# Where a two-layer mixer block computes its modulation vectors: from VectorE alone to TensorE in layer 0

## The chip, the core and the metric

One core of one Trainium2 chip runs the whole program as one launch. The metric is the device time of one execution in microseconds. Five engines work beside each other: TensorE (PE in the profile, with its weight loads as PEld), VectorE (DVE), ScalarE (ACT), GpSimd (POOL) and SyncE (SP), which here only issues transfers.

## The reference, cut to what matters

Two layers work on 256 context rows and 256 latent rows of width 1024. Each layer first turns two conditioning vectors (`c` and `c_ctx`, one row each) into six modulation vectors of 1024 (shift, scale and gate for the mixer, then for the feed-forward part):

```
sc_, scc = silu(c), silu(c_ctx)
mx_ = sc_ @ w_ada[l] + b_ada[l]          # 1024 x 6144 weights, 24 MB a layer
mc_ = scc @ w_ada[l] + b_ada[l]
sx1, ax1, gx1, sx2, ax2, gx2 = split(mx_, 6)
hx = rmsnorm(x, g_pre_mix[l]) * (1 + ax1) + sx1
yc, yx = token_mixer(hc, hx, ...)        # mLSTM, HGRN2 and differential attention on projections h @ w_in
x = x + gx1 * rmsnorm(yx, g_post_mix[l])
hx = rmsnorm(x, g_pre_ffn[l]) * (1 + ax2) + sx2
x = x + gx2 * rmsnorm(swiglu(hx, ...), g_post_ffn[l])
```

The context rows go the same way in layer 0 and are only read in layer 1, so layer 1 needs both vectors for its first two parts and only the latent one for the rest.

## The kernel before, in words

Rows sit 128 to a tile (four tiles: context 0 and 1, latent 2 and 3). All large products run on TensorE in three passes: weights are split into a rounded part and a rest (`whi`, line 295 on ScalarE; `wlo`, line 296 on VectorE), the activations `hT` likewise, and line 300 issues hi·hi, lo·hi and hi·lo. Weights come in blocks of 512 KB or less through a ring of three raw buffers (`wload`, loads issued by SP at line 292) into two split buffers each.

The stages of a layer, in the order of the program: a first projection; HGRN2 (`hg_proj`, `hg_mix`, heads in pairs, lines 735 to 866), whose mixing is a chain of small matmuls, copies on ScalarE and products on VectorE; the attention's projections (evacuated at line 904 with a bias row that SP loads at line 621); the attention itself (`da_tile`, lines 958 to 995), run in lockstep with mLSTM's decay factors (`ml_W`); mLSTM's projections; mLSTM (`ml_half`); the output projection; the feed-forward part.

The program is not executed in that order on each engine. The framework plans the engines' instruction streams ahead: at each point of its plan an engine takes the instruction that stands earliest in the program among those it deems ready, so later projections (line 300) fill the holes of the mixers. On the chip every engine, and SP's queue, then runs its own stream strictly in that order and waits where an operand is late.

**Modulation before.** The columns of layer 0's first two vectors are computed by TensorE in the opening stage (`first_mod`, line 489), as each `lhsT` is the 32-column block of `csil` that holds the two conditioning vectors. All others come from `ada_group` (line 195), a generator that is advanced by `ada_step` once for each weight block of a projection. A step loads 128 rows by 1024 columns of `w_ada` (512 KB, line 210, ring `araw` of two) and adds it, times one scalar for each partition, onto an accumulator of 128 x 1024 for each of the one or two vectors (`kinds`): line 224 for the first, line 226 for the others, on VectorE. After eight steps a gather on TensorE (line 231) sums the accumulator over partitions by multiplying with a 0/1 selector of 32 columns, into 32-partition strips of a PSUM bank of its own (`psa`), and VectorE adds the bias (line 233). Gate vectors are multiplied by their norm gain on GpSimd and put in DRAM; the others are transposed (line 247).

Layer 0's groups 1 (mixer gate) and 2 (feed-forward shift and scale) run during layer 0's mixers; their accumulators take the place of the residual rows `R`, which are loaded a second time afterwards (`load_rows`, line 1179). Group 3 (feed-forward gate) and layer 1's groups 0 to 3 are appended at line 1211, and their steps belong to the feed-forward part, though the plan starts the first of them earlier.

The eight PSUM banks are four for projections (`mm`), three for mixers (`mx`) and one for the modulation. The profile writes one float32 matmul as two instructions, so the counts of lines 231 and 489 are twice the program's.

Of the kernel before, what the change touches and what calls it, by code (L numbers as in the profile page):

```python
# [10 lines left out]
F32 = mybir.dt.float32  # L11
# [4 lines left out]
ALU = mybir.AluOpType  # L16
AX = mybir.AxisListType

P = 128
D = 1024  # L20
# [55 lines left out]

NPT = 2

NMM = 4

HP1, AHEAD = 20, 2000
# [18 lines left out]
def dit_block(ctx: ExitStack, tc: tile.TileContext, x, c, ctx_in, c_ctx, w_ada, b_ada, g_pre_mix,  # L100
# [12 lines left out]
    sm = pool("sm", 2)  # L113
    stg = pool("stg")
    psm = pool("psm", NMM, space=bass.MemoryType.PSUM)
    psx = pool("psx", 7 - NMM, space=bass.MemoryType.PSUM)
    psa = pool("psa", 1, space=bass.MemoryType.PSUM)
    drp = pool("drp", 1, space=bass.MemoryType.DRAM)

    uid = [0]  # L120
# [74 lines left out]
    def ada_group(l, g, place):  # L195


        c01 = ADA_COLS[g]
        kinds = (0, 1) if l < DEPTH - 1 or g == 0 else (0,)
        ns = 2 * len(c01)  # L200
        ba = par.tile([P, 512], F32, tag="ba", name=nm("ba"))
        G.memset(ba, 0.0)
        for r in range(2):
            for i, c0 in enumerate(c01):
                SY.dma_start(out=ba[64 * i + r:64 * i + r + 33:32, :], in_=b_ada[l, c0:c0 + D].rearrange("(j n) -> j n", j=2))
        todo = [(i, k) for i in range(len(c01)) for k in range(KD)]

        def load(i, k):
            raw = wp.tile([P, D], F32, tag="araw", name=nm("araw"), bufs=2)
            SY.dma_start(out=raw, in_=w_ada[l, k * P:(k + 1) * P, c01[i]:c01[i] + D])  # L210
            return raw

        raws = [load(*todo[0])]
        accs = {}
        for n_, (i, k) in enumerate(todo):
            if n_ + 1 < len(todo):
                raws.append(load(*todo[n_ + 1]))
            raw = raws.pop(0)
            if k == 0:
                accs[i] = place(kinds)  # L220
            for r in kinds:
                a = accs[i][r]
                if k == 0:
                    V.tensor_scalar_mul(a, raw, csil[:, k, r:r + 1])
                else:
                    V.scalar_tensor_tensor(out=a, in0=raw, scalar=csil[:, k, r:r + 1], in1=a, op0=ALU.mult, op1=ALU.add)  # L226
            yield
        ps = psa.tile([P, 512], F32, tag="ada", name=nm("ada"))
        for r in kinds:
            for j in range(ns):  # L230
                PE.matmul(ps[32 * j:32 * j + 32, :], lhsT=esel[:, r, :], rhs=accs[j // 2][r][:, (j % 2) * 512:(j % 2 + 1) * 512],
                          start=r == 0, stop=r == kinds[-1], skip_group_check=True)
        V.tensor_add(ba[:32 * ns], ps[:32 * ns], ba[:32 * ns])
        if g % 2:
            gp = par.tile([64, 512], F32, tag="gp", name=nm("gp"))
            G.memset(gp, 0.0)
            for r in range(2):
                SY.dma_start(out=gp[r:r + 33:32, :], in_=(g_post_mix, g_post_ffn)[g // 2][l].rearrange("(j n) -> j n", j=2))
            G.tensor_tensor(gp, gp, ba[:64], op=ALU.mult)
            gd = drp.tile([2, D], F32, tag=f"gd{l}{g}", name=nm("gd"))  # L240
            for j in range(2):
                G.dma_start(out=gd[:, j * 512:(j + 1) * 512], in_=gp[32 * j:32 * j + 2, :])
            ggd[l, g // 2] = gd
        else:
            pt = pst([P, 4, P])
            for c_ in range(4):
                PE.transpose(pt[:, c_, :], ba[:, c_ * P:(c_ + 1) * P], ident)
            cm = par.tile([P, 4, 4, 2], F32, tag=f"adaC{g}", name=nm("adaC"))
            V.tensor_copy(cm, vap(pt, 0, [[P, 4], [32, 4], [1, 2]]))
            adaC[l, g] = cm  # L250
        yield


# [20 lines left out]
    def ada_flush():  # L274
        while pending:
            ada_step_now()
# [201 lines left out]
    def first_mod(k):  # L478
        aw = aw0
        if k > 0:  # L480
            aw = ep.tile([P, KD, 2, P], F32, tag="aw", name=nm("aw"), bufs=4)
            for i in range(2):
                load_aw(aw, k, i)
        if k % 2 == 0:
            w0s[k // 2] = wload(first_src(0)[k // 2], eng=G)
        ps = psa.tile([P, 256], F32, tag="ada", name=nm("ada"))
# [106 lines left out]
    for l in range(DEPTH):  # L593
# [3 lines left out]
        q0 = qt[0] * P  # L597
        halves = (1, 0) if full else (1,)
        if full:

            turn = [0]

            def place0(kinds):
                turn[0] ^= 2
                return {r: res.tile([P, D], F32, tag=f"R{turn[0] + r}", name=nm("acc")) for r in kinds}
            pending += [ada_group(0, g, place0) for g in (1, 2)]
        mst = ExitStack()
        Y = {t: yp.tile([P, D], F32, tag=f"Y{t}", name=nm("Y")) for t in qt}
        mix = mst.enter_context(tc.tile_pool(name=f"mix{l}", bufs=1, reuse_waits="tile"))

        class Bias:

            def __init__(self, parts, p_, bufs=1):
                self.parts, self.row, self.pool, self.bufs = parts, None, p_, bufs

            def load(self):
                if self.row is None:
                    self.row = self.pool.tile([P, 512], F32, tag="brow", name=nm("brow"), bufs=self.bufs)
                    o = 0
                    for p in self.parts:  # L620
                        SY.dma_start(out=self.row[:, o:o + p.shape[-1]], in_=p.partition_broadcast(P))
                        o += p.shape[-1]

            def __getitem__(self, sl):
                return self.row[sl]
# [28 lines left out]
        hst = ExitStack()  # L654
        hg = hst.enter_context(tc.tile_pool(name=f"hg{l}", bufs=1, reuse_waits="tile"))
        Vhg = hg.tile([P, 4, 256], F32, tag="Vhg", name=nm("Vhg"))
        b0 = Bias([b_in[l, c0:c0 + n] for c0, n in first_cols] + [ml_f_bias[l]], hg)
        if l == 0:
            b0.row = b0_first

        def b0_load():
            if l > 0:
# [205 lines left out]
        ml_gates()  # L868
        lockstep(hg_mix(0), hg_mix(1))
        hg_out(0)  # L870
        bg = Bias([b_in[l, O_HGV + 256:O_HGV + 512]], hg)

        def ev_g(tt, ps):

# [153 lines left out]
        def chain(*gens):  # L1028
            for g in gens:
                yield from g  # L1030

        def spaced(gen, n):

            for _ in gen:
                for _ in range(n):
                    yield

        w_all = spaced(chain(*[ml_W(h, 1) for h in range(ML_H)]), WSP)
        if full:
            lockstep(chain(da_tile(2), da_tile(0)), chain(da_tile(3), da_tile(1)), w_all)  # L1040
        else:
            lockstep(da_tile(2), da_tile(3), w_all)
        def ev_v(t, ps, bb):
            V.tensor_tensor(Vml[:, t, :, :ML_D], ps.rearrange("p (h d) -> p h d", h=ML_H), bb.rearrange("p (h d) -> p h d", h=ML_H),
                            op=ALU.add)
# [156 lines left out]
        if l + 1 < DEPTH:  # L1202
            accq = stg.tile([P, 4, 768], F32, tag="qk", name=nm("accq"))
            turn1 = [0]

            def place1(kinds):
                turn1[0] ^= 1
                if turn1[0]:
                    return {r: vap(accq, D * r, [[1, D]]) for r in kinds}
                return {r: ff.tile([P, D], F32, tag="acc", name=nm("acc")) if r else vap(accq, 2 * D, [[1, D]]) for r in kinds}  # L1210
            pending += [ada_group(l, 3, place1)] + [ada_group(l + 1, g, place1) for g in range(4)]
        with tc.tile_pool(name=f"ff{l}", bufs=1, reuse_waits="tile") as ff:
            y_T(halves[-1], (0, 1))
            out_rest(halves[-1])
# [102 lines left out]
```

## Time and profile before

| | us |
|---|---|
| median of three runs | 1362.05 |
| lowest and highest of them | 1360.01, 1362.66 |
| the profiled execution, its own time | 1362.45 |
| its span in the trace | 1360.7 |
| TensorE busy | 1273.4 |
| VectorE busy | 895.8 |
| ScalarE busy | 609.0 |
| GpSimd busy | 197.7 |

The span is the stretch from the first to the last recorded instruction; the profiled execution's own time is 1.75 us longer than that. The mean granted TensorE clock is 0.975 of full speed.

How to read it: a busy time is the union of an engine's instructions, and a matmul counts until its result is out, so back-to-back matmuls overlap. Waits are put down to what came last by the trace.

### The profile page before, as it was taken

The numbers are of one execution on the slowest core, as the hardware profiler recorded it, in microseconds if no ns is written. First come the engines' busy times: TensorE is split into PE (matmuls) and PEld (weight loads), VectorE is DVE, ScalarE is ACT, GpSimd is POOL, SyncE is SP. The second block draws the span as 40 slices with busy tenths as digits, with TensorE's granted clock in tenths as the row PEclk, the third lists the DMA queues.
The fourth block names the chain that finished last, engine by engine and source line by source line (L and its number), as shares of the span: only waits on it lengthen the run. The fifth ranks groups of instructions, "written<-read, shape, count | busy, mean of one in ns | idle before, by whom it ended". The sixth has DMA issues, their size and how long they took to land. (4 is left out here: it accounts for less than half of the span.)

```text
span 1360.7 us, 21798 instructions
## 1 busy us (share of the span) xinstructions
PE 1273.4 (94%) x8414; PEld 1071.2 (79%) x8414; DVE 895.8 (66%) x1552; ACT 609.0 (45%) x1147; POOL 197.7 (15%) x304
## 2 busy tenths in 40 slices
PE   7998995999999899999999999899889998999997
PEld 5776874778878698788887887777787796899996
DVE  4899996665688898576436347667837666555555
ACT  3436451458544563222221236546425745544443
POOL 3123202111242300001000003132111111000001
PEclk9999997999999899999999999899889999899999
DMA  9872525222334577587425334531332424466563
GB/s 279 247 210 64 171 76 160 64 73 75 125 101 139 180 225 253 159 260 242 132 93 181 99 109 146 137 103 45 83 94 61 119 78 130 118 185 186 186 187 123
DMA packets 144309, 193.96 MB, mean 143 GB/s; under 512 B 10604, under 2 KB 110230, under 8 KB 144206
## 3 DMA queue, kind: packets, MB, share of 16 engines
q1 hardware_dynamic: 142782, 188.89, 46.0%
q0 software_dynamic: 1424, 3.68, 0.8%
q8 instruction: 66, 1.08, 0.3%
q14 instruction: 37, 0.30, 0.1%
HBM read 191.47 MB, written 1.08 MB: 142 GB/s over the span
## 5 line engine op out<-in xcount | busy, mean ns | idle before, releaser
L295 ACT CAST whi<-wraw 128x1024 fp32r<-128x1024 f32 (+3 forms) x259 | 259.2, 1001 | 456.4 <-PE mm L300 432.5
L296 DVE TENSOR_TENSOR wlo<-wraw,whi 128x1024 fp32r<-128x1024 f32 (+3 forms) x255 | 298.4, 1172 | 212.9 <-PE mm L300 115.6
L300 PE MATMUL mm<-hT,whi 128*128 128x256 f32 (+1 forms) x1920 | 357.1, 337 | 1.7 <-ACT whi L295 0.6
L300 PEld LDWEIGHTS mm<-hT,whi 128*128 128x128 f32 x1920 | 296.9, 192 | 41.7 <-issue 4.0
L300 PE MATMUL mm<-whi,hT 128*128 128x384 f32 (+4 forms) x1152 | 262.9, 358 | 10.3 <-DVE qk L904 5.0
L300 PEld LDWEIGHTS mm<-whi,hT 128*128 128x128 f32 x1152 | 198.8, 192 | 43.2 <-issue 12.1
L300 PE MATMUL mm<-hT,wlo 128*128 128x256 f32 (+1 forms) x960 | 185.5, 335 | 0.0
L300 PEld LDWEIGHTS mm<-hT,wlo 128*128 128x128 f32 x960 | 150.4, 191 | 17.6 <-issue 0.4
L300 PE MATMUL mm<-wlo,hT 128*128 128x384 f32 (+4 forms) x576 | 140.3, 353 | 0.0
L300 PE MATMUL mm<-whi,GT 128*128 128x512 f32 x504 | 127.4, 392 | 0.5 <-ACT whi L295 0.5
L300 PEld LDWEIGHTS mm<-whi,GT 128*128 128x128 f32 x504 | 93.6, 188 | 22.4 <-ACT whi L295 2.2
L300 PEld LDWEIGHTS mm<-wlo,hT 128*128 128x128 f32 x576 | 100.7, 191 | 12.0 <-issue 5.7
L226 DVE SCALAR_TENSOR_TENSOR accq<-araw,csil,accq 128x1024 f32<-128x1024 f32 x63 | 80.9, 1294 | 27.7 <-DMA araw<-in_w_ada_dram 27.4
L300 PE MATMUL mm<-wlo,GT 128*128 128x512 f32 x252 | 67.9, 389 | 0.0
L226 DVE SCALAR_TENSOR_TENSOR acc<-araw,csil,acc 128x1024 f32<-128x1024 f32 x49 | 62.9, 1307 | 4.1 <-DMA araw<-in_w_ada_dram 4.0
L300 PEld LDWEIGHTS mm<-wlo,GT 128*128 128x128 f32 x252 | 47.3, 188 | 9.9
L410 POOL TENSOR_SCALAR rstd<-hss 128x1 f32<-128x1 f32 (+2 forms) x44 | 19.6, 444 | 221.1 <-ACT hsq L634 139.1
L1249 DVE TENSOR_TENSOR sg<-sg,mm 128x256 f32<-128x256 f32 (+1 forms) x48 | 24.8, 519 | 34.6 <-PE mm L300 33.9
L411 POOL TENSOR_TENSOR rstd<-rstd,mhalf 128x1 f32<-128x1 f32 (+2 forms) x58 | 46.2, 797 | 4.7
L1273 POOL TENSOR_TENSOR Z<-Z,gg 128x512 f32<-128x512 f32 x6 | 8.9, 1491 | 234.2 <-ACT sqz L1272 234.2
L973 ACT ACTIVATE e<-mx,damx 128x512 f32<-128x512 f32 (+1 forms) x48 | 29.3, 616 | 26.0 <-DVE damx L970 25.9
L968 DVE TENSOR_REDUCE damx<-mx 128x1 f32<-128x512 f32 (+1 forms) x48 | 28.1, 597 | 18.8 <-PE mx L966 18.2
(275 smaller groups left out, 1466.3 us busy)
## 6 DMA issues: line engine op xcount, KB each, us to landing
araw<-in_w_ada_dram SPq DMA_DIRECT2D x80, 512.0 KB
wraw<-in_w_ffn_down_dram SPq DMA_DIRECT2D x50, 512.0 KB
wraw<-in_w_ffn_gate_dram SPq DMA_DIRECT2D x48, 512.0 KB
wraw<-in_w_ffn_up_dram SPq DMA_DIRECT2D x48, 512.0 KB
wraw<-in_w_in_dram SPq DMA_DIRECT2D x36, 512.0 KB
wraw<-in_w_in_dram SPq DMA_DIRECT2D x36, 384.0 KB
wraw<-in_w_out_dram SPq DMA_DIRECT2D x24, 512.0 KB
aw<-in_w_ada_dram SPq DMA_DIRECT2D x16, 512.0 KB
```

The costliest lines, as they stand in the source:

```text
L226: V.scalar_tensor_tensor(out=a, in0=raw, scalar=csil[:, k, r:r + 1], in1=a, op0=ALU.mult, op1=ALU.add)
L295: S.copy(hi[:, :nk, :n], raw[:, :nk, :n])
L296: (eng or V).tensor_tensor(lo[:, :nk, :n], raw[:, :nk, :n], hi[:, :nk, :n], op=ALU.subtract)
L300: PE.matmul(ps, lhsT=lhs, rhs=rhs, start=first, stop=last, skip_group_check=True)
L410: G.tensor_scalar(o[:, :width], ss, 1.0 / n, EPS, ALU.mult, ALU.add)
L411: G.tensor_tensor(o[:, :width], o[:, :width], mhalf[:, :width], op=ALU.pow)
L968: V.reduce_max(mx[:, j:j + 1], ps[:, :nk], axis=AX.X)
L973: S.activation(e[:, j, :nk], pp[j][:, :nk], AF.Exp, bias=mx[:, 2 + j:3 + j], scale=sc, accum_out=mx[:, 4 + j:5 + j])
L1249: V.tensor_mul(sg[:, :n], sg[:, :n], ps)
L1273: (V if cb else G).tensor_tensor(zs, zs, gg[1 if t < 2 else 0][:, cs_], op=ALU.mult)
```

## The change

Layer 0's four modulation vectors that are not computed in the opening stage go back to TensorE, in a new generator `ada_group0`: it takes two column blocks at once, loads 128 x 512 pieces (256 KB, ring of four) and issues for each a float32 matmul with `csil[:, k, :]` (32 columns) as `lhsT`, four pieces into the four 32-partition strips of one `mx` bank, accumulated over the eight steps k. Both gates (group 0) are stepped from the projections, one step for every second weight block (`pace[1] = 2`); shift and scale of the feed-forward part (group 1) are stepped from the attention's lockstep, one step for each three rounds. There is no accumulator in SBUF, so `R` stays and the second `load_rows` goes.

Layer 1's groups stay on VectorE, with loads and products cut into halves of 512 columns (ring of four) and two further steps (`LAG`) between the last product and the gather. They now come first in the feed-forward part, as layer 0's group 3 is gone from there.

The modulation's own PSUM bank becomes a fourth `mx` bank, which opening stage, gathers and `ada_group0` share with the mixers. Two bias rows move: layer 1's first one to `yp`'s tile `Y0`, HGRN2's gate bias to the staging tile `qk`.

```diff
-    psx = pool("psx", 7 - NMM, space=bass.MemoryType.PSUM)
-    psa = pool("psa", 1, space=bass.MemoryType.PSUM)
+    psx = pool("psx", 8 - NMM, space=bass.MemoryType.PSUM)
...
-        todo = [(i, k) for i in range(len(c01)) for k in range(KD)]
+        todo = [(i, k, h) for i in range(len(c01)) for k in range(KD) for h in range(2)]
...
-            raw = wp.tile([P, D], F32, tag="araw", name=nm("araw"), bufs=2)
+            raw = wp.tile([P, 512], F32, tag="araw", name=nm("araw"), bufs=4)
...
+            if h:
+                yield
+        for _ in range(LAG):
             yield
-        ps = psa.tile([P, 512], F32, tag="ada", name=nm("ada"))
+        ps = pst([P, 512])
...
+    def ada_group0(g):
+
+        c01 = ((2 * D, 5 * D), (3 * D, 4 * D))[g]
...
+        ps = pst([P, 512])
+        for k in range(KD):
+            for j in range(4):
+                raw = wp.tile([P, 512], F32, tag="araw", name=nm("araw"), bufs=4)
+                SY.dma_start(out=raw, in_=w_ada[0, k * P:(k + 1) * P, c01[j // 2] + (j % 2) * 512:c01[j // 2] + (j % 2) * 512 + 512])
+                PE.matmul(ps[32 * j:32 * j + 32, :], lhsT=csil[:, k, :], rhs=raw, start=k == 0, stop=k == KD - 1, skip_group_check=True)
+            if k < KD - 1:
+                yield
+        V.tensor_add(ba, ps, ba)
+        if g == 0:
+            for i in range(2):
+                gate_store(0, i, ba, i)
+        else:
+            norm_cols(0, 2, ba)
+        yield
...
-            pending += [ada_group(0, g, place0) for g in (1, 2)]
+            pending.append(ada_group0(0))
+            pace[1] = 2
...
-        b0 = Bias([b_in[l, c0:c0 + n] for c0, n in first_cols] + [ml_f_bias[l]], hg)
-        if l == 0:
-            b0.row = b0_first
+        b0 = Bias([b_in[l, c0:c0 + n] for c0, n in first_cols] + [ml_f_bias[l]],
+                  row=b0_first if full else yp.tile([P, D], F32, tag="Y0", name=nm("b0")))
...
-        bg = Bias([b_in[l, O_HGV + 256:O_HGV + 512]], hg)
+        bg = Bias([b_in[l, O_HGV + 256:O_HGV + 512]], row=vap(stg.tile([P, 4, 768], F32, tag="qk", name=nm("bg")), 0, [[1, 256]]))
...
+        ada_flush()
+        ada_rest = spaced(ada_group0(1), 2) if full else iter(())
...
-            lockstep(chain(da_tile(2), da_tile(0)), chain(da_tile(3), da_tile(1)), w_all)
+            lockstep(chain(da_tile(2), da_tile(0)), chain(da_tile(3), da_tile(1)), ada_rest, w_all)
...
+        for _ in ada_rest:
+            pass
...
-        if full:
-            load_rows()
...
-            pending += [ada_group(l, 3, place1)] + [ada_group(l + 1, g, place1) for g in range(4)]
+            pending += [ada_group(l + 1, g, place1) for g in range(4)]
+            pace[1] = 1
```

## Rows read from the trace of the kernel before

**Rows 1.** Page of the profile, part 1: engines over the whole span
```profile
PE 1273.4 (94%) x8414; PEld 1071.2 (79%) x8414; DVE 895.8 (66%) x1552; ACT 609.0 (45%) x1147; POOL 197.7 (15%) x304
```

**Rows 2.** Windows: stretch, length, PE PEld DVE ACT POOL busy (instructions), PEclk, DMA, GB/s
```profile
55.00:205.00 150.00, 141.34 (x1618) 111.69 (x1619) 142.01 (x239) 74.49 (x135) 31.68 (x27) 0.99 0.45 137
205.00:225.00 20.00, 5.82 (x21) 2.49 (x21) 16.18 (x28) 2.53 (x3) 7.44 (x9) 0.70 0.61 186
225.00:365.00 140.00, 136.69 (x738) 112.38 (x737) 78.17 (x189) 78.65 (x200) 23.04 (x55) 0.99 0.26 77
365.00:480.00 115.00, 106.55 (x589) 87.76 (x588) 94.70 (x193) 60.74 (x143) 38.50 (x54) 0.94 0.47 150
480.00:845.00 365.00, 362.18 (x1755) 299.81 (x1755) 220.19 (x243) 117.52 (x157) 18.24 (x20) 1.00 0.55 174
845.00:1160.00 315.00, 285.36 (x2030) 243.54 (x2028) 202.86 (x444) 164.73 (x356) 57.44 (x101) 0.95 0.34 95
```

**Rows 3.** Who waited for whom, TensorE, 55 to 370 us: total, times, longest
```profile
PE ada L231 <- DVE acc L226: 14.2, 1, 14.2
...
PE mx L798 <- ACT Ck L789: 3.7, 3, 2.4
```

**Rows 4.** Timeline around 210 us, all engines: start, length, engine, line, operation
```profile
198.91 10.04 SPq L210 DMA_DIRECT2D araw<-in_w_ada_dram  x4
...
215.24 0.90 SPq L621 DMA_DIRECT2D brow<-in_b_in_dram  x2
...
219.30 0.33 SPq L210 DMA_DIRECT2D araw<-in_w_ada_dram  x1
...
222.05 2.48 DVE L904 TENSOR_TENSOR qk<-mm,brow 128x512 f32<-128x512 f32 x4
...
222.18 1.93 PE L231 MATMUL ada<-acc,esel 128*32 128x512 f32 x6 [14.19 <-DVE acc L226]
...
224.04 5.11 PE L300 MATMUL mm<-whi,hT 128*128 128x512 f32 x16
...
230.80 3.79 PE L300 MATMUL mm<-whi,hT 128*128 128x512 f32 x16
```

**Rows 5.** Timeline, the same place in layer 1
```profile
994.58 2.50 PE L300 MATMUL mm<-whi,hT 128*128 128x320 f32 x8 [5.01 <-DVE qk L904]
```

**Rows 6.** Busy time by stretch of line 226 alone
```profile
55.00:250.00 195.00, 53.97 (x42) 0.96 0.45 137
250.00:480.00 230.00, 20.26 (x16) 0.97 0.36 111
```

**Rows 7.** Busy time of line 231 alone, all of layer 0's groups
```profile
100.00:460.00 360.00, 10.11 (x32) 1.46 (x32) 0.97 0.35 107
```

**Rows 8.** Timeline at 572 us, a gather of eight matmuls in one run
```profile
571.86 1.06 PE L231 MATMUL ada<-accq,esel 128*32 128x512 f32 x8
...
573.71 1.21 PE L300 MATMUL mm<-whi,GT 128*128 128x512 f32 x4
```

**Rows 9.** Timeline of TensorE, gathers among softmax rounds (280 us) and alone (444 us)
```profile
279.96 1.06 PE L231 MATMUL ada<-acc,esel 128*32 128x512 f32 x6
...
280.94 0.80 PE L300 MATMUL mm<-whi,hT 128*128 128x384 f32 x3
...
444.44 1.04 PE L231 MATMUL ada<-accq,esel 128*32 128x512 f32 x2
...
445.42 0.73 PE L300 MATMUL mm<-whi,hT 128*128 128x512 f32 x2
```

**Rows 10.** Who waited for whom, VectorE, 55 to 250 us
```profile
DVE acc L226 <- DMA araw<-in_w_ada_dram: 4.0, 4, 1.6
DVE acc L224 <- DMA araw<-in_w_ada_dram: 0.6, 1, 0.6
```

**Rows 11.** Who waited for whom, TensorE, 370 to 850 us
```profile
PE mx L439 <- DVE nsc L447: 2.1, 1, 2.1
...
PE mm L300 <- DVE hT L1133: 1.4, 1, 1.4
```

More of the change, by code (lines that the diff above doesn't have):

```diff
@@ L77 @@
 NPT = 2
+LAG = 2
 NMM = 4
@@ L205, in ada_group, with load @@
                 SY.dma_start(out=ba[64 * i + r:64 * i + r + 33:32, :], in_=b_ada[l, c0:c0 + D].rearrange("(j n) -> j n", j=2))
-        todo = [(i, k) for i in range(len(c01)) for k in range(KD)]
-        def load(i, k):
-            raw = wp.tile([P, D], F32, tag="araw", name=nm("araw"), bufs=2)
-            SY.dma_start(out=raw, in_=w_ada[l, k * P:(k + 1) * P, c01[i]:c01[i] + D])
+        todo = [(i, k, h) for i in range(len(c01)) for k in range(KD) for h in range(2)]
+        def load(i, k, h):
+            raw = wp.tile([P, 512], F32, tag="araw", name=nm("araw"), bufs=4)
+            SY.dma_start(out=raw, in_=w_ada[l, k * P:(k + 1) * P, c01[i] + 512 * h:c01[i] + 512 * h + 512])
             return raw
-        raws = [load(*todo[0])]
+        raws = [load(*x_) for x_ in todo[:3]]
         accs = {}
-        for n_, (i, k) in enumerate(todo):
-            if n_ + 1 < len(todo):
-                raws.append(load(*todo[n_ + 1]))
+        for n_, (i, k, h) in enumerate(todo):
+            if n_ + 3 < len(todo):
+                raws.append(load(*todo[n_ + 3]))
             raw = raws.pop(0)
-            if k == 0:
+            if k == h == 0:
                 accs[i] = place(kinds)
             for r in kinds:
-                a = accs[i][r]
+                a = accs[i][r][:, 512 * h:512 * h + 512]
                 if k == 0:
@@ L234, in ada_group @@
         if g % 2:
[L235 to L242, printed above, removed]
@@ L243, in ada_group, with gate_store @@
-            ggd[l, g // 2] = gd
-        else:
[L245 to L250, printed above, removed]
+            gate_store(l, g // 2, ba, 0)
+        else:
+            norm_cols(l, g, ba)
+        yield
+    def gate_store(l, which, ba, i):
+        o = 64 * i
+        gp = par.tile([P, 512], F32, tag="gp", name=nm("gp"))
+        G.memset(gp, 0.0)
+        for r in range(2):
+            SY.dma_start(out=gp[o + r:o + r + 33:32, :], in_=(g_post_mix, g_post_ffn)[which][l].rearrange("(j n) -> j n", j=2))
+        G.tensor_tensor(gp[o:o + 64], gp[o:o + 64], ba[o:o + 64], op=ALU.mult)
+        gd = drp.tile([2, D], F32, tag=f"gd{l}{which}", name=nm("gd"))
+        for j in range(2):
+            G.dma_start(out=gd[:, j * 512:(j + 1) * 512], in_=gp[o + 32 * j:o + 32 * j + 2, :])
+        ggd[l, which] = gd
@@ new lines, in norm_cols @@
+    def norm_cols(l, g, ba):
+        pt = pst([P, 4, P])
+        for c_ in range(4):
+            PE.transpose(pt[:, c_, :], ba[:, c_ * P:(c_ + 1) * P], ident)
+        cm = par.tile([P, 4, 4, 2], F32, tag=f"adaC{g}", name=nm("adaC"))
+        V.tensor_copy(cm, vap(pt, 0, [[P, 4], [32, 4], [1, 2]]))
+        adaC[l, g] = cm
+    def ada_group0(g):
+        c01 = ((2 * D, 5 * D), (3 * D, 4 * D))[g]
+        ba = par.tile([P, 512], F32, tag="ba", name=nm("ba"))
+        G.memset(ba, 0.0)
+        for r in range(2):
+            for i, c0 in enumerate(c01):
+                SY.dma_start(out=ba[64 * i + r:64 * i + r + 33:32, :], in_=b_ada[0, c0:c0 + D].rearrange("(j n) -> j n", j=2))
+        ps = pst([P, 512])
[12 more added lines that the diff above has]
+            norm_cols(0, 2, ba)
@@ L485, in first_mod @@
             w0s[k // 2] = wload(first_src(0)[k // 2], eng=G)
-        ps = psa.tile([P, 256], F32, tag="ada", name=nm("ada"))
+        ps = pst([P, 256])
         for i in range(2):
@@ L599, in dit_block @@
         if full:
[L601 to L605, printed above, removed]
-            pending += [ada_group(0, g, place0) for g in (1, 2)]
+            pending.append(ada_group0(0))
+            pace[1] = 2
         mst = ExitStack()
@@ L611, in dit_block, with __init__ @@
         class Bias:
-            def __init__(self, parts, p_, bufs=1):
-                self.parts, self.row, self.pool, self.bufs = parts, None, p_, bufs
+            def __init__(self, parts, p_=None, bufs=1, row=None):
+                self.parts, self.row, self.pool, self.bufs = parts, row, p_, bufs
             def load(self):
@@ L618, in load @@
                     self.row = self.pool.tile([P, 512], F32, tag="brow", name=nm("brow"), bufs=self.bufs)
[L619 to L622, printed above, removed]
+                o = 0
+                for p in self.parts:
+                    SY.dma_start(out=self.row[:, o:o + p.shape[-1]], in_=p.partition_broadcast(P))
+                    o += p.shape[-1]
             def __getitem__(self, sl):
```

## The prediction, made before the change was run

> **What bounds the kernel now.** I read the page's first part, then the busy times cut by stage, then TensorE's waits, then the timeline where one wait stood out. TensorE is busy for 94% of the span [rows 1], and an average like that hides where the rest lies, so the stages matter [rows 2]. Layer 0's mixers run from 55 to 365 us: in the HGRN2 stretch TensorE is busy for 141.34 of 150 us and VectorE for 142.01, both nearly full; then come 20 us in which TensorE works for 5.82; in the attention it is full again. The feed-forward part of layer 0 has TensorE at 362.18 of 365 us with VectorE at 220.19: there TensorE alone is the bound. So work taken off VectorE pays only in the HGRN2 stretch and in the hole behind it, and work put on TensorE costs its full time nearly everywhere.
>
> The hole is one wait: a gather at line 231 stood 14.2 us for the last products of line 226 [rows 3]. The timeline shows why [rows 4]: SP's queue was held from 198.91 on by four `araw` loads, each waiting for a buffer that VectorE had not yet read, so the products came late, and the bias row for the next projections went out only at 215.24. Behind it TensorE's clock was on its lower level (1.2 of 2.4 GHz) for a while: sixteen matmuls of line 300 took 5.11 us at 224.04 and 3.79 at 230.80.
>
> **Step by step**, against the profiled execution's own 1362.45 us, which is 0.4 over the median.
>
> *Removed from TensorE: the gathers of layer 0.* The groups' 32 instructions are busy for 10.11 us [rows 7]. Starts show a run of 1.06 us to take 0.98 until the next matmul starts [rows 9], so 10.11 x 0.93 = **-9.4**. Bounds: -10.1 to -7, if some of them filled holes.
>
> *Removed from VectorE: layer 0's products.* 53.97 us between 55 and 250 us, 20.26 after it [rows 6]. First, the wait of 14.2 us goes. What is late next is the evacuation at line 904, at 222.05 in the same place [rows 4]; it needs the bias row, which no longer queues behind loads that wait for VectorE. Layer 1 has the same chain without any modulation, and TensorE still waited 5.01 us for it [rows 5]. I take that as what stays: **-9.2**; bounds -14.2 (and the slow clock's 1.3 on top) and 0. Second, TensorE's other idle time in the HGRN2 stretch, 150 - 141.34 = 8.7 us, is mostly waits for ScalarE and VectorE in the mixers' chain, as the 3.7 us at line 798 [rows 3]. With 54 of VectorE's 142 + 16 us gone the chain waits less in its queue, but ScalarE's copies stay in it: half, **-4.3**; bounds -8.7 and 0. Third, the 20.26 us after 250 us [rows 6] are group 3's, and layer 1's group 0, with as many products for each load, moves into their place. In halves each holds VectorE for about half as long, and TensorE waited there for VectorE's lines 447 and 1133 for 3.5 us [rows 11]: a third of it, **-1.0**; bounds -3.5 and +1.
>
> *Added to TensorE: 64 float32 matmuls in 16 steps of four.* The nearest row is the gather at 572 us, the same shape (32 columns in, 512 moving, four strips): its sixteen instructions, eight matmuls, held TensorE from 571.86 until line 300 went on at 573.71 [rows 8], 1.85 us or 0.93 for four. The four strips evidently run beside each other, since a lone matmul, two instructions, took 0.98 [rows 9]. 16 x 0.93 = **+14.8** if each step stays in one piece. In one piece is the nearer end, as a gather of three matmuls ran unbroken among softmax rounds at 279.96 [rows 9]. The far end, all 64 alone, is 62.7.
>
> *Added: TensorE waits for the loads.* Until now a late `araw` held VectorE; now it holds TensorE's stream, and behind it the projections and mixers, and behind those the splits of `whi` and `wlo` and SP's next weight loads. VectorE waited 4.6 us in all for late pieces here [rows 10]. With no lead beyond one step I take them as fully uncovered on TensorE: **+4.6**; bounds 0, where a step's loads have the two weight blocks before it as cover, and 14.7, one wait of the mean length, 4.6 / 5 = 0.92 us, at each of 16 steps.
>
> *Moved or doubled, at nothing.* SP issues 64 pieces here instead of 24 of twice the size, at 0.33 us each [rows 4], 13 us spread over 310, covered by the weight ring's lead; if that lead were gone they would delay weights by as much. Their wait is now for a matmul of the step before, not for VectorE. Group 3's 4 MB move from the feed-forward part into the mixers and the four reloads of `R` (2 MB) go: net 2 MB more, and the attention's stretch, which takes the second half, moved only 77 GB/s [rows 2]. Layer 1's products in halves double VectorE's instructions in the feed-forward part; the cover is the 145 us that VectorE is idle there [rows 2]. GpSimd's gate products grow by little and it is idle most of the time. The fourth mixer bank is taken by `ada_group0` during layer 0's HGRN2 and attention, so the mixers have three there as before; in layer 1 TensorE's idle 29.6 us of 315 [rows 2] show no wait for a bank. I take 0 for it, bounds -3 and +2; for the shared bank in the opening stage and the moved bias rows 0, bounds -1 and +1, as a re-planned order can move either.
>
> Sum: -9.4 - 9.2 - 4.3 - 1.0 + 14.8 + 4.6 = -4.5, so 1362.45 - 4.5 = **1358.0**.
>
> **Rivals.**
> 1. *The mixers run through.* VectorE's relief is worth its far bounds: -10.1 - 14.2 - 1.3 - 8.7 - 3.5 + 14.8 = -23.0, 1339.5. For it speaks that VectorE was at 95% through the HGRN2 stretch; against it the 5.01 us in layer 1, where VectorE has no modulation.
> 2. *The steps fall to pieces* (the slower side). Each of the four matmuls waits for its own load, and in the attention's lockstep a step outranks the projections that fill the holes, so the plan may start each matmul when its piece lands, with projections between. Then the eight steps of the second group cost 4 x 0.98 each instead of 0.93: 8 x 2.99 = +24, 1382; with half of them split, 1370. It decides from the second split step on, as each takes back 3.0 of the 4.5 us gained. Against it: the unbroken gather at 280 us, though its operands came ready together. The lone matmul's 0.98 us includes whatever a change of shape costs. The Trainium skill (TensorEngine Tiling (Array Packing), Tiling Modes) says that going from one tiling mode to another drains TensorE; by that rule every split pays two more drains. The trace agrees as far as it goes: a single matmul of 512 columns costs more than a quarter of four.
> 3. *Late loads.* Every step waits once, at the mean length above: 14.7 instead of 4.6, +10.1, 1368.1. For it: the steps have no prefetch of their own, and SP's queue blocks on a weight buffer at any time. Against: two weight blocks of matmuls lie between steps.
> 4. *The hole stays.* The evacuation at line 904 keeps its place in VectorE's order behind a wait of another kind, and TensorE stands as long: +9.2, 1367.2. The change then doesn't do what taking products off VectorE says.
>
> **How the numbers follow.** A measurement of this kernel can tell some 0.2% from no change, 2.7 us. Chances: forecast 0.45, rivals 0.20, 0.15, 0.12 and 0.08. The forecast's own range, from the nearer bounds of its terms, is 1350 to 1365: of its 0.45 some 0.31 are faster, 0.10 the same, 0.04 slower. Rival 1 is all faster; of the others' 0.35, 0.08 fall within 0.2% (few steps split or late) and 0.27 beyond. Faster 0.51, same 0.18, slower 0.31. The range leaves out the far end of rival 1 and rival 2 with all steps split: 1342 to 1374.
>
> **What would show it.** Right: the matmuls of `ada_group0` in sixteen runs of eight instructions, about 1 us each; no wait of TensorE above 6 us between 200 and 230 us; line 231 with 32 instructions, all after layer 0's mixers; the feed-forward part as long as before. Wrong: runs of two instructions in the attention (rival 2), a group of TensorE waits for `araw` of over 10 us (rival 3), a wait for line 904 of 10 us or more (rival 4), or the HGRN2 stretch ending over 10 us earlier (rival 1). A longer feed-forward part, or layer 1's mixers shifted by over 5 us, would mean that the parts taken at nothing were not.

## The result, and the profile after

The change made the kernel slower: a median of 1376.99 us in four runs (1371.70 to 1378.78) against 1362.36 (1360.01 to 1365.10), a ratio of 1.0108 with a 95% interval of 1.0084 to 1.0131. The forecast was 1358.0 with a range of 1342 to 1374, so the time lies outside the range, on the side of rival 2. The profiled execution took 1378.78 us, its span 1377.1.

The engines over the span, after (page, part 1), to be held against [rows 1]:

```profile
span 1377.1 us, 22143 instructions
...
PE 1295.5 (94%) x8510; PEld 1075.7 (78%) x8510; DVE 834.2 (61%) x1551; ACT 597.7 (43%) x1140; POOL 177.3 (13%) x303
```

VectorE lost 61.6 us of work, as meant. TensorE gained 22.1 us of busy time, of which the forecast had 14.8 - 9.4 = 5.4. The stages tell where. I cut both traces at the same instructions: the transpose that ends the opening stage, the first matmuls of the attention and of mLSTM, the first product of the feed-forward part, and the last output transpose of layer 1's HGRN2. Busy times by stretch (columns as in [rows 2]), after:

```profile
0.00:61.80 61.80, 50.26 (x338) 35.40 (x338) 32.21 (x73) 18.90 (x31) 16.61 (x30) 1.00 0.91 249
61.80:250.90 189.10, 175.81 (x1780) 133.10 (x1779) 112.13 (x238) 81.25 (x143) 30.63 (x46) 0.96 0.38 113
250.90:387.80 136.90, 132.94 (x702) 97.18 (x701) 72.18 (x177) 67.50 (x191) 19.52 (x53) 1.00 0.41 123
387.80:501.90 114.10, 104.98 (x626) 90.38 (x625) 95.72 (x210) 65.19 (x150) 31.27 (x49) 0.97 0.44 138
501.90:1004.70 502.80, 486.92 (x2840) 403.58 (x2838) 309.79 (x492) 191.32 (x309) 50.26 (x60) 0.98 0.48 144
1004.70:1377.10 372.40, 344.62 (x2234) 316.10 (x2233) 212.15 (x364) 173.57 (x319) 28.99 (x65) 0.97 0.46 134
```

and the first three of the kernel before, cut in the same way:

```profile
0.00:51.10 51.10, 41.25 (x325) 32.05 (x326) 26.64 (x68) 17.12 (x28) 15.55 (x27) 1.00 0.97 269
51.10:247.10 196.00, 172.00 (x1746) 134.41 (x1745) 168.75 (x292) 83.73 (x146) 42.40 (x45) 0.96 0.47 144
247.10:365.00 117.90, 114.59 (x644) 94.21 (x643) 71.02 (x177) 75.47 (x197) 21.36 (x53) 1.00 0.24 70
```

Beside them the forecast's own terms, sorted into these stretches (gathers by where line 231 is busy before: 5.91, 1.06 and 3.14 us; the 4.6 us of waits for loads in two halves):

| stretch | before | after | difference | forecast |
|---|---|---|---|---|
| opening | 51.1 | 61.8 | +10.7 | 0 |
| HGRN2 | 196.0 | 189.1 | -6.9 | 7.4 - 5.5 - 9.2 - 4.3 + 2.3 = -9.3 |
| attention | 117.9 | 136.9 | +19.0 | 7.4 - 1.0 + 2.3 = +8.7 |
| mLSTM | 118.4 | 114.1 | -4.3 | -2.9 - 1.0 = -3.9 |
| feed-forward, layer 1's HGRN2 | 505.9 | 502.8 | -3.1 | 0 |
| rest | 371.4 | 372.4 | +1.0 | 0 |
| sum | 1360.7 | 1377.1 | +16.4 | -4.5 |

So 20.9 us separate forecast and result, and two stretches hold 21.0 of them: the opening with 10.7 and the attention with 10.3.

**The opening.** TensorE's timeline, before: each of the eight groups of line 489 (sixteen instructions, eight matmuls of 256 columns) stands in one run.

```profile
48.43 1.07 PE L489 MATMUL ada<-aw,csil 128*32 128x256 f32 x16
49.43 0.45 PE L300 MATMUL mm<-wlo,hT 128*128 128x400 f32 x1
```

After (the line is now 525), the last group comes in five runs, between other transposes. Of the other seven groups one comes in one run, one in four, and five in two, of one matmul and of seven.

```profile
52.30 0.63 PE L525 MATMUL mx<-aw,csil 128*32 128x256 f32 x4
52.86 0.33 PE L536 MATMUL mx<-ident,ar 128*128 128x128 f32 x1
53.12 0.62 PE L525 MATMUL mx<-aw,csil 128*32 128x256 f32 x2
53.66 0.33 PE L536 MATMUL mx<-ident,ar 128*128 128x128 f32 x1
```

A run of one or two matmuls holds TensorE for some 0.55 us until the next instruction starts (52.30 to 52.86 with two, 53.12 to 53.66 with one). The whole of eight takes 1.0 (48.43 to 49.43). Busy time of this line alone, before and after:

```profile
0.00:55.09 55.09, 9.43 (x128) 3.52 (x128) 1.00 0.98 277
```
```profile
0.00:65.17 65.17, 15.37 (x128) 4.51 (x128) 1.00 0.89 244
```

These windows end where the first HGRN2 projection starts, 10.1 us later than before. 5.9 of it are this line, with twenty runs in place of eight; most of the rest is a wait of 3.1 us for HGRN2's first evacuation (line 698). The stretches of the table are cut elsewhere: twelve matmuls of the first projection, some 2.5 us, stand behind the cut before and ahead of it after, so that in the table the opening looks longer and HGRN2 shorter by as much.

**The attention.** TensorE's timeline there, after (line 278 is the new matmul, two instructions each):

```profile
263.97 1.07 PE L278 MATMUL mx<-araw,csil 128*32 128x512 f32 x8 [1.21 <-ACT e L1003]
264.96 0.38 PE L1039 MATMUL mx<-Mp,ident 128*128 128x256 f32 x1
...
282.57 1.05 PE L278 MATMUL mx<-araw,csil 128*32 128x512 f32 x2
283.54 0.45 PE L336 MATMUL mm<-whi,hT 128*128 128x384 f32 x1
...
293.81 2.44 PE L278 MATMUL mx<-araw,csil 128*32 128x512 f32 x6
```

A run takes 0.99 us with four matmuls (263.97 to 264.96) and 0.97 with one (282.57 to 283.54): it is paid by the run, not by the matmul. Two runs lasted longer, as their matmuls waited for pieces of weights on the way: 1.31 us at 275.90 and 2.37 at 293.81, together 1.7 us more than two others. The first step stands in one piece; behind it the steps fall apart, and the group's 32 matmuls stand in nineteen runs instead of eight. (The lockstep advances the group in every second of its rounds, `spaced(..., 2)`, not in every third.) From each run's start to the next instruction, which is the forecast's measure, the first group (nine runs, in HGRN2) took 8.4 us and the second 20.4. Their busy time, which also counts the overlap with that next instruction, in HGRN2 and in the attention:

```profile
61.80:250.90 189.10, 9.60 (x64) 1.43 (x64) 0.96 0.38 113
250.90:387.80 136.90, 21.66 (x64) 3.09 (x64) 1.00 0.41 123
```

**The hole.** TensorE's waits between 61 and 251 us, after, to be held against [rows 3]:

```profile
PE mm L336 <- DVE qk L934: 7.2, 1, 7.2
PE mm L336 <- DVE Vhg L698: 3.1, 1, 3.1
PE mx L828 <- ACT Ck L819: 1.2, 4, 0.4
```

The 14.2 us at line 231 are gone, the waits for `Ck` shrank, and 7.2 us remain at the evacuation (line 904 before, now 934). Its bias row was late again, behind other waits. The waits of SP's queue between 190 and 230 us, and a timeline of the same place:

```profile
SPq L250 <- DMA gd<-gp: 13.8, 1, 13.8
...
SPq L272 <- POOL ba L269: 4.4, 1, 4.4
```
```profile
213.18 1.03 SPq L250 DMA_DIRECT2D gp<-in_g_post_ffn_dram  x2
...
221.13 0.83 SPq L652 DMA_DIRECT2D brow<-in_b_in_dram  x2
...
225.14 0.26 DVE L947 TENSOR_TENSOR lp<-lv 128x96 f32<-128x96 f32 x1 [2.10 <-DMA lv<-in_da_lambda_dram]
...
225.60 2.47 DVE L934 TENSOR_TENSOR qk<-mm,brow 128x512 f32<-128x512 f32 x4
...
226.43 6.47 PE L336 MATMUL mm<-whi,hT 128*128 128x512 f32 x16 [7.21 <-DVE qk L934]
...
234.58 3.79 PE L336 MATMUL mm<-whi,hT 128*128 128x512 f32 x16
```

The first group ends with both gates, one after the other through a single buffer `gp`. The second gate's gain can be loaded only when the first gate's store is through. SP stood 13.8 us for that, and 4.4 more until GpSimd had cleared `ba` for the second group, with the bias row of line 652 behind both. There is a second chain, in VectorE's own stream: just ahead of the evacuation stands a product of the attention's lambda vectors (line 947). GpSimd issued their load at 220.96, behind its work for the second gate, and VectorE stood 2.1 us for it. The trace does not say when the bias row landed, so which of the two came last is open.

Behind the hole TensorE's clock was mostly on the lower of its two levels (1.2 and 2.4 GHz): 0.56 of full speed was granted from 226.43 to 232.74, and the sixteen matmuls took 6.47 us where the next sixteen took 3.79. Before, behind the longer wait, they took 5.11 [rows 4]. So the hole became 7.0 us shorter and the slow matmuls behind it 1.4 longer in this execution.

### The profile page after: what moved, and what is told of

Same layout as the page of the kernel before. It is cut to its first block, busy times and chain, and to the rows that moved or that the text cites. A ratio compares the mean times of both kernels' runs of the same rounds, so it can differ in the third digit from the quotient of the medians.

```text
span 1377.1 us, 22143 instructions
## 1 busy us (share of the span) xinstructions
PE 1295.5 (94%) x8510; PEld 1075.7 (78%) x8510; DVE 834.2 (61%) x1551; ACT 597.7 (43%) x1140; POOL 177.3 (13%) x303
## 4 chain that ended last, share of the span: by engine, by line
PE 79%; DVE 6%; ACT 6%; POOL 3%; issue 3%; DMA 2%; SPq 0%; DVEq 0%; POOLq 0%; ACTq 0%
PE mm L336 64%; PE mx L1136 2%; PE mx L278 2%; PE mx L996 1%; DVE wlo L332 1%; POOL rstd L447 1%; ACT whi L331 1%; PE mx L1018 1%; DMA wraw<-in_w_ffn_down_dram 1%; ACT Ck L819 1%; PE mm L1124 1%; PE mx L525 1%; POOL Kh L844 1%; PE mx L1012 1%; PE mx L475 1%
## 5 line engine op out<-in xcount | busy, mean ns | idle before, releaser
L332 DVE TENSOR_TENSOR wlo<-wraw,whi 128x1024 fp32r<-128x1024 f32 (+3 forms) x255 | 297.7, 1168 | 274.7 <-PE mm L336 167.2
L336 PE MATMUL mm<-whi,hT 128*128 128x384 f32 (+4 forms) x1152 | 261.1, 358 | 18.2 <-DVE qk L934 12.2
L336 PEld LDWEIGHTS mm<-hT,wlo 128*128 128x128 f32 x960 | 150.4, 191 | 17.5 <-issue 0.4
L227 DVE SCALAR_TENSOR_TENSOR accq<-araw,csil,accq 128x512 f32<-128x512 f32 x98 | 70.8, 747 | 11.5 <-DMA araw<-in_w_ada_dram 11.2
L447 POOL TENSOR_TENSOR rstd<-rstd,mhalf 128x1 f32<-128x1 f32 (+2 forms) x58 | 42.5, 732 | 4.7
L819 ACT COPY Ck<-Kh 128x512 f32<-128x512 f32 (+1 forms) x56 | 28.6, 524 | 22.6 <-DVE Kh L844 15.4
L446 POOL TENSOR_SCALAR rstd<-hss 128x1 f32<-128x1 f32 (+2 forms) x44 | 13.8, 314 | 190.8 <-ACT hsq L665 155.5
```

Source lines behind the costliest of these rows:

```text
L332: (eng or V).tensor_tensor(lo[:, :nk, :n], raw[:, :nk, :n], hi[:, :nk, :n], op=ALU.subtract)
L336: PE.matmul(ps, lhsT=lhs, rhs=rhs, start=first, stop=last, skip_group_check=True)
L446: G.tensor_scalar(o[:, :width], ss, 1.0 / n, EPS, ALU.mult, ALU.add)
L447: G.tensor_tensor(o[:, :width], o[:, :width], mhalf[:, :width], op=ALU.pow)
L819: S.copy(C[:, q0:].rearrange("p (a b i) -> p b a i", b=2, i=m), vap(K_, 2 * m * pq0, [[512 + m, 2], [2 * m, np_], [1, m]]))
```

## The experiments

Each run was compared with the kernel before on the same chip. The changed kernel was not timed again beside them, so a difference from its median is one between sessions; the kernel before lay between 1361.43 and 1362.50 us in all of these. Lengths of stretches are from the profiled execution of each.

**1. The shared bank alone.** The kernel before, with its modulation bank put into the mixers' pool and nothing else of the change.

```diff
-    psx = pool("psx", 7 - NMM, space=bass.MemoryType.PSUM)
-    psa = pool("psa", 1, space=bass.MemoryType.PSUM)
+    psx = pool("psx", 8 - NMM, space=bass.MemoryType.PSUM)
...
-        ps = psa.tile([P, 512], F32, tag="ada", name=nm("ada"))
+        ps = pst([P, 512])
...
-        ps = psa.tile([P, 256], F32, tag="ada", name=nm("ada"))
+        ps = pst([P, 256])
```

> The kernel before with one part of the change alone: the modulation's own PSUM bank becomes the fourth mixer bank, and opening stage and gathers take theirs from the mixers' pool. Theory (the shared bank breaks up the opening's modulation matmuls and costs about 10 us there): the first HGRN2 projection starts near 65 us instead of 55, and the whole time is 1370 to 1374 us, 8 to 12 more than before. Rival (the later opening comes from the other parts, such as the earlier pieces of modulation weights in SP's queue): start near 55 us, 1360 to 1364 us.

Measured: 1372.45 us (1370.35 to 1373.97) against 1361.43, ratio 1.0070 (1.0054 to 1.0087). Its opening, and in it the busy time of line 488 (489 before):

```profile
0.00:62.10 62.10, 49.98 (x338) 35.27 (x338) 32.36 (x73) 19.73 (x32) 16.45 (x30) 1.00 0.89 248
```
```profile
0.00:65.17 65.17, 15.08 (x128) 4.41 (x128) 1.00 0.87 242
```

The bank alone makes the opening 11.0 us longer, with the groups broken up as after the change; HGRN2 and attention stay about as before (195.2 and 119.5 against 196.0 and 117.9).

**2. The whole change, the opening's own bank kept.** Three mixer banks and one for the modulation until the opening ends, four mixer banks from there on.

```diff
-    psx = pool("psx", 8 - NMM, space=bass.MemoryType.PSUM)
+    pso = ExitStack()
+    psx = pso.enter_context(tc.tile_pool(name="psx0", bufs=7 - NMM, space=bass.MemoryType.PSUM))
+    psa = pso.enter_context(tc.tile_pool(name="psa0", bufs=1, space=bass.MemoryType.PSUM))
...
     V.tensor_copy(cols, prow)
+    pso.close()
+    psx = pool("psx", 8 - NMM, space=bass.MemoryType.PSUM)
```

> The changed kernel with three mixer banks and one of its own for the modulation during the opening stage only, and four mixer banks from then on. Theory: the opening ends where it did before (projection from 55 to 56 us), everything behind is as in the changed kernel but 10 us earlier: 1365 to 1369 us. Rival (the opening is late for another reason): start near 65 us, 1375 to 1379 us. A second rival (the fourth bank itself slows a later stage): the start is right but the gain is gone later, 1371 or more.

Measured: 1366.24 us (1364.70 to 1369.58), ratio 1.0031 (1.0021 to 1.0041). Opening, HGRN2 and attention:

```profile
0.00:51.30 51.30, 40.92 (x325) 31.73 (x326) 27.62 (x67) 17.12 (x28) 16.15 (x27) 1.00 1.01 275
51.30:238.60 187.30, 175.90 (x1794) 133.31 (x1792) 114.87 (x244) 83.15 (x146) 32.31 (x49) 0.98 0.40 121
238.60:375.00 136.40, 132.59 (x702) 97.17 (x701) 72.14 (x177) 67.48 (x191) 19.46 (x53) 1.00 0.40 124
```

The opening is back at 51.3 and the attention is as long as after the change. Both sides agree: the shared bank costs some 11 us in the opening, and the rest of the loss is elsewhere. Why the plan orders the opening's matmuls so when the banks are shared was not tested.

**3. Each step held together by force.** The four matmuls of a step are put into one critical section, so that the plan can place nothing between them.

```diff
             for j in range(4):
-                raw = wp.tile([P, 512], F32, tag="araw", name=nm("araw"), bufs=4)
+                raws[j] = wp.tile([P, 512], F32, tag="araw", name=nm("araw"), bufs=4)
...
-                PE.matmul(ps[32 * j:32 * j + 32, :], lhsT=csil[:, k, :], rhs=raw, start=k == 0, stop=k == KD - 1, skip_group_check=True)
+            with tc.tile_critical():
+                for j in range(4):
+                    PE.matmul(ps[32 * j:32 * j + 32, :], lhsT=csil[:, k, :], rhs=raws[j], start=k == 0, stop=k == KD - 1, skip_group_check=True)
```

> The changed kernel with the four matmuls of a step of layer 0's modulation held together as one piece in the plan. Theory (a run costs 1 us whether it has one matmul or four, and the second group's eight steps had fallen into 19 runs): 16 runs of eight instructions, 11 fewer, and 9 to 13 us less in the attention, 1364 to 1369 us. Rival (the attention is longer by the added work and its waits for loads, not by the pieces): TensorE waits for the last piece instead, the attention is shorter by 3 us at most, 1373 to 1378 us.

Measured: 1391.26 us (1390.36 to 1391.93), ratio 1.0209 (1.0194 to 1.0224): a miss for both sides, as the edit changed more than the order. The new matmuls in the attention took 9.39 us instead of 21.66, yet its stretch was 139.8 us long:

```profile
260.70:400.50 139.80, 9.39 (x64) 1.30 (x64) 0.96 0.36 112
```
```profile
286.65 1.07 PE L281 MATMUL mx<-araw,csil 128*32 128x512 f32 x8 [1.73 <-POOL rstd L450]
```

The first line is the busy time of the new matmuls, the second a step in the timeline. TensorE stood before each of the sixteen sections, 0.43 to 1.75 us and 18.2 in all, mostly for instructions that the matmuls do not use, as `rstd` here; in the changed kernel it stood before one run, for 1.2. HGRN2's stretch was 197.7 us, 8.6 longer than after the change; 8.5 of the 18.2 stand there. The run shows what the matmuls cost in one piece, and nothing about the time of a kernel in which they stay together.

**4. The same aim by the order of the loads.** The pieces are loaded from the last to the first, the matmuls keep their order: the first matmul's piece comes last, and when it is there, so are the others.

```diff
-            for j in range(4):
-                raw = wp.tile([P, 512], F32, tag="araw", name=nm("araw"), bufs=4)
+            for j in (3, 2, 1, 0):
+                raws[j] = wp.tile([P, 512], F32, tag="araw", name=nm("araw"), bufs=4)
...
-                PE.matmul(ps[32 * j:32 * j + 32, :], lhsT=csil[:, k, :], rhs=raw, start=k == 0, stop=k == KD - 1, skip_group_check=True)
+            for j in range(4):
+                PE.matmul(ps[32 * j:32 * j + 32, :], lhsT=csil[:, k, :], rhs=raws[j], start=k == 0, stop=k == KD - 1, skip_group_check=True)
```

> The changed kernel with the four loads of a step issued in the reverse order of its matmuls, so that the first matmul waits for the last load and the others then stand ready. In the planned order the second group has 10 runs instead of 19, and nothing else of that group changes. Theory (each run costs about 1 us whatever it holds): the stretch from the first transposes of the attention's keys to the first of mLSTM's, 136.9 us in the changed kernel, falls by 8 to 10 us; 1367 to 1370 us. Rival (the length comes from the work and from waits for loads): 134 us or more, 1374 to 1379 us.

Measured: 1374.08 us (1372.33 to 1376.46), ratio 1.0098 (1.0074 to 1.0122). The new matmuls in HGRN2 and attention:

```profile
62.50:253.30 190.80, 9.60 (x64) 1.43 (x64) 0.96 0.36 112
253.30:380.70 127.40, 10.60 (x64) 1.52 (x64) 1.00 0.42 132
```

Ten runs instead of nineteen, 10.60 us instead of 21.66, and the attention is 9.5 us shorter. The mechanism is shown. The time expected of it is not: the medians differ by 2.9 us and the profiled executions by 6.0 (1378.78 to 1372.76), as opening, HGRN2, mLSTM and the feed-forward part each took back 0.7 to 1.7 us. Runs of the changed kernel spread over 7 us, so how much of the 9.5 us arrives at the end stays open here.

**5. Both gates from one buffer.** The gains of both gates are loaded into the two halves of one `gp`, multiplied once, and stored, so that SP does not wait for a store.

```diff
-            for i in range(2):
-                gate_store(0, i, ba, i)
+            gates_store0(ba)
...
+        for i in range(2):
+            for r in range(2):
+                SY.dma_start(out=gp[64 * i + r:64 * i + r + 33:32, :], in_=(g_post_mix, g_post_ffn)[i][0].rearrange("(j n) -> j n", j=2))
+        G.tensor_tensor(gp, gp, ba, op=ALU.mult)
```

> The changed kernel with both gate vectors of layer 0 multiplied and stored from one tile in one go, so that the second does not wait for the first one's store. Theory (SP's queue stood 13.8 us for that store, and the attention's bias row behind it): SP does not stand there, the bias row goes out before 210 us, TensorE's wait of 7.2 us for line 904's evacuation falls to 2 to 5 us, 1372 to 1375 us. Rival (the evacuation waits in VectorE's order behind the load of the lambda vectors anyway): the wait stays at 6 to 8 us, 1375 to 1379 us.

Measured: 1373.74 us (1370.19 to 1377.42), ratio 1.0083 (1.0056 to 1.0110). HGRN2's stretch went from 189.1 to 184.3 us, and the hole from 7.2 to 2.9; TensorE's wait for it in this kernel:

```profile
PE mm L349 <- DVE qk L947: 2.9, 1, 2.9
```

So the two gates in a row through one buffer cost 4.3 us of the hole. By which chain is not parted: the bias row goes out at 217.24 instead of 221.13, though SP still stands 8.5 us for `ba`, and the plan also puts the evacuation (222.35) ahead of the lambda product (224.74). The stretch is 4.8 us shorter; the medians differ by 3.3, less than the 7 us over which the runs of either kernel spread.

**6. The second group elsewhere.** With the opening and the gates repaired, could the second group leave the attention? First, both groups stepped from the layer's projections, one step for every block:

```diff
-            pending.append(ada_group0(0))
-            pace[1] = 2
+            pending += [ada_group0(0), ada_group0(1)]
...
-        ada_rest = spaced(ada_group0(1), 2) if full else iter(())
```

> The changed kernel with own bank in the opening only, both gates from one tile, and the second group of layer 0 stepped from the projections behind the first group, one step for every weight block, so that none is left for the attention. Theory: the attention's stretch is back at 118 to 121 us, the HGRN2 stretch is 8 to 10 us longer by eight whole steps; 1353 to 1360 us. Rival (twice the loads for each block make TensorE wait for pieces in the HGRN2 stretch): waits for loads of over 10 us there, 1364 or more.

Measured: 1360.70 us in one run. The attention is back at 116.3 us, but HGRN2 took 201.8, 17.5 more than with experiment 5's and not 8 to 10, and the 64 new matmuls 25.75 us there: the cost moved with them. Second, the second group stepped from mLSTM's projections:

```diff
-        ada_rest = spaced(ada_group0(1), 2) if full else iter(())
...
+        if full:
+            pending.append(ada_group0(1))
```

> The changed kernel with own bank in the opening only, both gates from one tile, and the second group stepped from mLSTM's projections, one step for every second block. Its steps then stand behind the attention in the program. In the planned order it has 13 runs. Theory of the runs: the second group costs 13 us, 1355 to 1360 us. Rival: as in the changed kernel, 17 to 19 us, 1362 to 1366 us.

Measured: 1382.46 us in one run, a miss: mLSTM's projections fill the attention's holes, so the plan put these steps there all the same. TensorE's waits between 51 and 400 us and its timeline:

```profile
PE mx L294 <- DMA araw<-in_w_ada_dram: 8.3, 6, 3.6
```
```profile
346.36 1.92 PE L294 MATMUL mx<-araw,csil 128*32 128x512 f32 x2 [3.63 <-DMA araw<-in_w_ada_dram]
```

Here rival 3 happened, late loads on TensorE, which the change itself does not show: there its weight loads for line 278 waited for pieces 2.6 us in five times.

**7. The repairs together.** Experiments 2, 4 and 5 in one kernel:

> The changed kernel with three repairs at once: own bank in the opening only, both gates from one tile, loads in reverse order. Theory (three separate costs of 10, 3 and 9 us): 1353 to 1358 us, below the kernel before by 4 to 8. Rival (the gains eat each other, as TensorE is full behind each of them): 1360 to 1366 us.

Measured: 1353.70 us (1347.03 to 1358.82) against 1362.50, ratio 0.9942 (0.9920 to 0.9964): faster than both kernels. Its opening, HGRN2 and attention:

```profile
0.00:51.70 51.70, 41.21 (x325) 32.02 (x326) 26.61 (x68) 17.11 (x28) 15.66 (x27) 1.00 0.99 272
51.70:233.50 181.80, 174.31 (x1792) 132.19 (x1791) 113.67 (x244) 83.06 (x146) 30.45 (x47) 1.00 0.40 124
233.50:361.00 127.50, 121.40 (x702) 95.39 (x701) 72.11 (x177) 67.41 (x191) 20.11 (x53) 1.00 0.41 132
```

Alone the three gave 10.7, 2.9 and 3.3 us of median, 16.9 in all; together they gave 23.3. In the profiled executions, where the changed kernel's was its slowest, they gave 14.1, 6.0 and 5.7, 25.8 in all, and together 28.3. So the medians of so few runs leave most of that gap open, and part of what remains is the clock and not the edits. Behind the same wait of 2.9 us the sixteen matmuls after the hole took 5.41 us in experiment 5 (granted clock 0.69), 3.89 here (1.00), and 5.50 in the run of this same kernel in experiment 8 (0.68):

```profile
223.18 5.41 PE L349 MATMUL mm<-whi,hT 128*128 128x512 f32 x16 [2.91 <-DVE qk L947]
```
```profile
211.68 3.89 PE L353 MATMUL mm<-whi,hT 128*128 128x512 f32 x16 [2.93 <-DVE qk L953]
```
```profile
212.17 5.50 PE L353 MATMUL mm<-whi,hT 128*128 128x512 f32 x16 [2.93 <-DVE qk L953]
```

**8. With and without the fourth bank.** The same repairs with the banks as before, three for the mixers and one for the modulation, beside the kernel of 7 again.

```diff
-    psx = pool("psx", 8 - NMM, space=bass.MemoryType.PSUM)
+    psx = pool("psx", 7 - NMM, space=bass.MemoryType.PSUM)
+    psa = pool("psa", 1, space=bass.MemoryType.PSUM)
...
-        ps = pst([P, 512])
+        ps = psa.tile([P, 512], F32, tag="ada", name=nm("ada"))
...
```

> The changed kernel with the loads reversed and both gates from one tile, and with the banks of the kernel before: three for mixers and one for the modulation throughout, so the fourth mixer bank is gone and with it its effect on the opening. Theory (the fourth bank gives the mixers nothing, as layer 0's modulation holds it and layer 1 shows no wait for a bank): within 3 us of the kernel with all three repairs measured beside it, 1351 to 1357 us. Rival (the fourth bank pays in the mixers once the opening is mended): slower than that kernel by 4 to 8 us, mostly in the HGRN2 and attention stretches.

> The kernel with all three repairs again, beside the one without a fourth bank: 1350 to 1357 us, below the kernel before by 5 to 12 us in the same runs.

Measured: without, 1355.06 us (1351.57 to 1366.01), ratio 0.9962 (0.9937 to 0.9987); with, 1350.87 (1350.25 to 1356.12), ratio 0.9930 (0.9906 to 0.9953). The fourth bank may be worth 4 us behind the opening, but the intervals overlap. It is not settled.

## Why the prediction was wrong, step by step

- **The shared bank in the opening stage, "0, bounds -1 and +1": wrong by 10.7 us.** This is the step that failed first, and the range failed with it. I priced the bank as a place and looked for waits for it. It is also an order: with one pool for all, line 525's groups stand between the transposes in twenty runs instead of eight. Experiments 1 and 2 show the cost from both sides, and with the opening mended the time, 1366.24 us, lies inside the range. That each added run costs about half a us is read from the timeline (12 more runs, 5.9 us more of this line); the 3.1 us at line 698 behind it were not taken apart. Behind that wait the clock was low too: sixteen matmuls from 65.17 took 5.29 us at a granted clock of 0.71, and 3.92 at 1.00 before.
- **"+14.8 if each step stays in one piece": wrong by 13.0 us in the second group.** 20.4 us for its eight steps instead of 7.4, of which 1.7 are waits for pieces; the first group, in nine runs, took 8.4. This is rival 2 at its place and at its price, about 1 us for each run too many: 24 us more for eight steps wholly split, and 11.3 for nineteen runs without their waits. That the whole time, 1377, falls between that rival's 1370 and 1382 is luck all the same, as half of what is too much came from the opening. I gave it 0.15 because a gather had run unbroken at 280 us [rows 9]; as I wrote there, that gather's operands were ready together. Experiment 4 makes a step's pieces ready together and the runs become ten. The rule that I cited for it (the Trainium skill, TensorEngine Tiling (Array Packing), Tiling Modes: changing the mode drains TensorE) fits, as a lone matmul lasts as long as four; but no run here parts the drain from the plain length of a matmul, since strips run beside each other.
- **The hole, "-9.2": too much by 2.2, and by 1.4 more of slow clock.** It shrank from 14.2 to 7.2, and the forecast left 5.0; the matmuls behind it lost 2.7 us to the clock, against 1.3 before. A bias row was late on SP's queue, as forecast, and the lambda vectors on GpSimd's, which the forecast did not have. The reason was new: I took GpSimd's gate products as growing "by little" and did not see that two gates in a row share one buffer, so that SP and GpSimd wait for a store. Experiment 5 shows that this cost 4.3 us, with 2.9 left, and not through which of the two queues.
- **The mixers' waits in HGRN2, "-4.3": about right.** TensorE's idle time in the stretch fell from 24.0 us to 13.3; 7.0 of it are the hole and 3.7 the chain and the rest, although the stretch now begins with the 3.1 us at line 698.
- **The waits for loads, "+4.6": too much.** 2.6 us, in the weight loads of line 278, of which 1.7 lengthened runs and stand in the 20.4 above; rival 3 did not come. Rival 4 came in part (7.2 us), rival 1 not: the HGRN2 stretch became 6.9 us shorter, 9.60 us of new work included.
- **The gathers, "-9.4": right**, as line 235 has its 32 instructions in the feed-forward part alone. **VectorE's third part, "-1.0": did not come.** TensorE's waits for the two VectorE lines (now 458 and 1168) came to 4.3 us in mLSTM's stretch, against 3.5. That this stretch is 4.3 us shorter where 3.9 were forecast is luck.
- **The parts taken at nothing in the feed-forward part** did cost nothing: 502.8 us against 505.9. Of the 3.1 us some 2 are 17 of its matmuls that now stand ahead of the cut, in mLSTM's stretch; the rest was not tested.

Put together: 10.7 for the opening, 13.0 + 1.0 for the steps, 2.2 for the hole and 1.4 for the clock behind it make 28.3 us too little; against it stand the 4.6 us of waits for loads, since those that came are in the steps, and 3.1 of the feed-forward part. That leaves 20.6 of the 20.9; smaller parts of either sign are not taken apart.

## What to carry to other kernels

When a planner orders the engines, price an edit of a buffer pool as an edit of the order, and read the runs of instructions in the new stream before any sum. Where an instruction costs by the run and not by the piece, as narrow matmuls in strips do here, see to it that all pieces of a run become ready at once: loading the piece that is used first last brought nineteen runs down to ten. And for every queue that runs in a fixed order, look at what waits for a buffer in front of the transfer that the next stage needs, stores included. Before an edit is credited with a few us, compare the granted clock of the two executions.

## What the runs showed of the hardware

A run of float32 matmuls with 32 output columns, each in a strip of its own, between full-width matmuls, holds TensorE about as long with one as with four: 0.97 us for one of 512 columns and 0.99 for four; some 0.55 us for one or two of 256 columns, and 1.0 for eight, two to a strip. I had known the price of a lone one from [rows 9], and not that the stream would be full of them.

The clock granted to the same instructions differs between executions of one kernel: behind a wait of 2.9 us sixteen matmuls took 3.89 us at 1.00 in one and 5.50 at 0.68 in another. The time of a whole execution goes with its mean granted clock: 1358.82 us at 0.977 and 1347.03 at 0.988 in experiment 7, 1378.78 at 0.977 and 1371.70 at 0.983 for the changed kernel.
